# Hybrid encoder step on one core: z of block 0 leaves PSUM by ScalarE, two query loads in place of eight, the last gate norm dealt between attention heads

## The chip, the cores and the metric

The kernel runs on one core of one Trainium2 chip. The time is the device time of one execution in microseconds (us), the median of several executions. TensorE (PE in the profile, PEld for its weight loads) multiplies matrices into PSUM, VectorE (DVE), ScalarE (ACT) and GpSimd (POOL) work element by element, and SyncE (SP) issues all DMA transfers of this kernel from one queue.

## The reference

One layer of a streaming encoder with 2048 new frames of one stream ("prompt") and 32 further frames of another stream that has 2048 cached positions ("sample"). Model width is 1024.

```python
h = x + rmsnorm(mixer(rmsnorm(x, g_mix_pre)), g_mix_post)
y = h + rmsnorm(conv_ffn(rmsnorm(h, g_ffn_pre)), g_ffn_post)

# mixer
proj = h @ w_in                       # q, k, v (8 heads x 64), z (512), x/B/C (768), dt (8)
attn = stick_breaking(q, k_all, v_all)      # w = sigmoid(z_qk) * prod of (1 - sigmoid) of later keys
y = ssd_scan(silu(dwconv(xbc)), softplus(dt), ...) + d_skip * x
y = rmsnorm(y * silu(z), g_ssm_out)         # the gate and the gate norm
out = concat([rmsnorm(attn, g_attn_out), y]) @ w_out
# conv_ffn
act = gelu(dwconv(gate)) * up;  out = act @ w_down
```

The results are both y, the new k and v rows, and the final scan and convolution states. Everything is float32; the kernel splits an operand into a high and a low part and takes three matmuls for a product.

## The kernel before, in words

The 2080 frames are cut into four blocks (`SBS`): three of 512 prompt frames, and a last one of 512 prompt frames and the 32 sample frames (544). Features lie on the partitions, frames on the free axis.

`phase_in` runs over the four blocks: input norm, the projections of x/B/C, v, k and q, the SSD scan, and for blocks 0 to 2 also the gate and its norm. In `gate`, each of four chunks of 128 features is a dense product of 24 matmuls in a PSUM bank named o (two banks, `kn.po`). The chunk's z is then put through a sigmoid, multiplied with itself and into the scan's output `xc`. Block 0 differs: its input norm factor r0 is not yet multiplied into x, so each projection is multiplied by r0 when it leaves PSUM. For z, VectorE does this at line 647 straight from the bank; blocks 1 and 2 copy z out by ScalarE at line 651 and need no factor. `gate_norm` then squares and sums the four chunks (lines 667 to 671), gets the reciprocal root, scales each chunk on VectorE (line 677), splits it (lines 681, 683) and stores the parts in DRAM (`yS`, lines 684 and 685).

A z chunk can only start when its bank is free, so with two banks the third chunk waits until the first has left PSUM.

Block 3's gate and gate norm are handed out as two generators (line 619). They run in the next stage, the attention of block 0. `Attention.heads` goes through "slots", one for each head, key block and 128 queries: 32 slots for block 0 (8 heads x 1 key block x 4), 64 for block 1, and so on. A slot computes scores on PE (lines 890, 894; tile z), two sigmoids on ScalarE (738, 739; gam and beta), a running product by a scan on VectorE (741), a product of these (746; POOL, or VectorE for one in five), transposes on PE (909; pt), a split by ScalarE and VectorE (913, 914; wt), and the value matmuls (931; pa). Between slots `fill` takes steps from a generator `filler`, at a rate of `steps / slots`. For block 0 the filler is block 3's gate: 32 steps of six matmuls each (128 x 256 or 272 wide), one a slot. At every third slot a step of `sample` (the sample frames' attention over the cached keys) is taken as well, ten in all. `sample` begins with a memset of its query tile qp on VectorE (761), then SP loads qp from DRAM, one load for each head (764), then the first keys (786). When the heads of block 0 are done, the rest of `sample` and the whole of block 3's gate norm follow.

Then `Tail` begins: block 0's attention output is normed (`norm_in`, lines 832 to 839), goes with yS through the output projection, a residual and a second norm, and the feed-forward, all as filler between the slots of block 1's heads.

The order of instructions on each engine is set by the tile framework's scheduler when the program is built. It may move an instruction ahead of others that it does not depend on. Filler matmuls are pinned behind the last attention matmul that was recorded before them (`pin`, `mark`); attention slots are not pinned behind filler, so the scheduler can take slots of the next heads first where it expects the filler to wait. On the chip each engine works through its list in order.

Of the kernel before, what the change touches and what calls it, by code (L numbers as in the profile page):

```python
# [8 lines left out]
F32 = mybir.dt.float32  # L9
# [3 lines left out]
ALU = mybir.AluOpType  # L13
# [18 lines left out]
P = 128  # L32
D = 1024
KC = D // P
SEQ = 2048
DEC = 32
# [228 lines left out]
def phase_in(kn, ctx):  # L265
# [101 lines left out]
    for s, (t0, nt) in enumerate(SBS):  # L367
# [250 lines left out]
        if last:  # L618
            return lambda tm, pool: (
                gate(kn, s, xs, xc, None, tm),  # L620
                gate_norm(kn, s, xc, tm, lambda sq, *r: kn.rstd_narrow(pool, *kn.bank, [sq], *r)),
            )
        bufs = {"khi": 2, "klo": 2, "t": 2, "sq": 1, "zc": 2}
        tm = lambda nm: (so if nm in ("khi", "klo") else tmp).tile([P, 550 if nm == "t" else 544], F32, name=nm, bufs=bufs[nm])
# [6 lines left out]
def gate(kn, s, xs, xc, r0, tm):  # L631

    nc, nt = kn.nc, SBS[s][1]
    tiles = tiles_of(nt)
    for c in range(4):
        w = kn.weight(kn.wp, kn.a["wz"][c], key=("z", c) if s < NSB - 1 else ("z", c, "part"))
        for c0, c1 in tiles:
            n = c1 - c0
            ps = kn.po.tile([P, 512], F32, name="o")
            for k in range(KC):  # L640
                kn.dense(ps, w[k : k + 1], xs, c0, c1, k0=k, first=k == 0, last=k == KC - 1, pin=s == NSB - 1)
                if len(tiles) == 1 or k % 2:
                    yield
            t = tm("t")
            if r0 is not None:
                z = tm("t")
                nc.vector.tensor_tensor(z[:, :n], ps[:, :n], r0[:, c0:c1], op=ALU.mult)
                ps = z
            elif s < NSB - 1:
                z = tm("zc")  # L650
                nc.scalar.copy(z[:, :n], ps[:, :n])
                ps = z
            nc.scalar.activation(t[:, :n], ps[:, :n], AF.Sigmoid)
            nc.vector.tensor_tensor(t[:, :n], ps[:, :n], t[:, :n], op=ALU.mult)
            e = min(c1, 512)
            nc.vector.tensor_tensor(xc[:, c, c0:e], xc[:, c, c0:e], t[:, : e - c0], op=ALU.mult)
            if c1 > 512:
                nc.gpsimd.tensor_tensor(xc[:, c, 512:544], xc[:, c, 515:547], t[:, e - c0 : n], op=ALU.mult)


def gate_norm(kn, s, xc, tm, rstd):

    nc, nt = kn.nc, SBS[s][1]
    sq = tm("sq")
    for c in range(4):
        if c == 0:
            nc.scalar.activation(sq[:, :nt], xc[:, c, :nt], AF.Square)
        else:
            t = tm("t")
            nc.scalar.activation(t[:, :nt], xc[:, c, :nt], AF.Square)  # L670
            nc.gpsimd.tensor_tensor(sq[:, :nt], sq[:, :nt], t[:, :nt], op=ALU.add)
        yield
    r = rstd(sq, nt, 512)
    for c in range(4):
        yield
        n = xc[:, c, :nt] if s == NSB - 1 else tm("zc")[:, :nt]
        nc.vector.scalar_tensor_tensor(
            n, xc[:, c, :nt], kn.col(C_GSSM + c), r[:, :nt], op0=ALU.mult, op1=ALU.mult
        )
        hi = tm("khi")[:, :nt].bitcast(F32R)  # L680
        nc.scalar.copy(hi, n)
        lo = tm("klo")[:, :nt].bitcast(F32R)
        nc.gpsimd.tensor_tensor(lo, n, hi.bitcast(F32), op=ALU.subtract)
        nc.sync.dma_start(kn.yS[s][0, :, c, :], hi.bitcast(F32))
        nc.sync.dma_start(kn.yS[s][1, :, c, :], lo.bitcast(F32))


class Attention:
# [60 lines left out]
    def sample(self, ctx, pu):  # L749
        kn, nc, a = self.kn, self.kn.nc, self.kn.a  # L750
        kp = ctx.enter_context(kn.tc.tile_pool(name="as_k", bufs=2, reuse_waits="tile", side="right"))
        mk = kp.tile([P, DEC], BF16, name="masks", bufs=1)
        nc.gpsimd.memset(mk[:], 0.0)
        for i in range(4):
            r = slice(32 * i, 32 * i + 32)
            nc.gpsimd.affine_select(
                out=mk[r, :], in_=mk[r, :], compare_op=ALU.is_gt, fill=NEG, base=0,
                pattern=[[-1, DEC]], channel_multiplier=1,
            )
        qp = kp.tile([P, 4, DH], F32, name="qp", bufs=1)  # L760
        nc.vector.memset(qp[:], 0.0)
        for h in range(NH):
            r = slice(64 * (h % 2), 64 * (h % 2) + 64)
            nc.sync.dma_start(qp[r, h // 2, 32 * (h % 2) : 32 * (h % 2) + 32], kn.qF[r, h // 2, :])
        own = []
        for g in range(2):
            own.append([kp.tile([P, w], F32, name=f"{nm}{g}", bufs=1) for nm, w in (("sgam", 513), ("sbeta", 512), ("sprow", 513))])
            nc.gpsimd.memset(own[g][0][:, 512:513], 1.0)
        carry = [kp.tile([P, 1], F32, name=f"scarry{g}", bufs=1) for g in range(2)]
        av = pu.tile([P, 512], F32, name="u")  # L770
        prev = [None, None]
        for kc in (4, 3, 2, 1, 0):
            n = DEC if kc == 4 else 512
            nsub = 1 if kc == 4 else 4
            v = [kp.tile([P, 512], F32, name="sv", bufs=4) for _ in range(nsub)]
            for i in range(nsub):
                if kc == 4:
                    nc.sync.dma_start(v[i][:DEC, :], kn.vF[:])
                else:
                    nc.sync.dma_start(v[i][:], a["cvv"][:, 4 * kc + i, :])  # L780
            for g in range(2):
                z = self.pz.tile([P, 512], F32, name="z")
                for i in range(2):
                    c = 2 * g + i
                    k = kp.tile([P, 512], F32, name="sk", bufs=2)
                    nc.sync.dma_start(
                        k[:, :n], kn.kF[:, c, :] if kc == 4 else a["ck"][c][:, 512 * kc : 512 * kc + 512]
                    )
                    nc.tensor.matmul(
                        z[DH * i : DH * i + DH, :n], qp[:, c, :], k[:, :n], start=True, stop=kc < 4  # L790
                    )
                if kc == 4:
                    nc.tensor.matmul(z[:, :n], kn.identb[:], mk[:], start=False, stop=True)
                w, end = self.weights_of(z[:, :n], n, prev[g], own[g])
                prev[g] = carry[g][:]
                nc.scalar.copy(prev[g], end)
                t = self.pt.tile([P, 512], F32, name="pt")
                q = min(n, P)
                for i in range(nsub):
                    nc.tensor.transpose(t[:q, P * i : P * i + P], w[:, P * i : P * i + q], kn.ident[:])  # L800
                wt = kp.tile([P, 512], F32, name="swt")
                nc.scalar.copy(wt[:q, : nsub * P], t[:q, : nsub * P])
                for i in range(nsub):
                    for e in range(2):
                        nc.tensor.matmul(
                            av[DH * e : DH * e + DH, P * g : P * g + P], wt[:q, P * i + DH * e : P * i + DH * e + DH],
                            v[i][:q, 256 * g + P * e : 256 * g + P * e + P],
                            start=kc == 4 and g == 0, stop=kc == 0 and g == 1 and i == 3, skip_group_check=True,
                        )
                yield  # L810
        self.att_s = self.cp.tile([P, 4, DEC], F32, name="att_s")
        for g in range(2):
            at = kp.tile([P, DH], F32, name="at")
            for hh in range(4):
                r = slice(32 * hh, 32 * hh + 32)
# [683 lines left out]
def build(nc, tc, a, o):  # L1499
    kn = Kernel(nc, tc, a, o)  # L1500
    with ExitStack() as ctx:
# [24 lines left out]
        att = Attention(kn, heads)  # L1526
        kn.bank = pu, "u"
        late = ssd.enter_context(tc.tile_pool(name="ssd_tmp", bufs=2, reuse_waits="tile", side="right"))
        att.filler, normed = rest(lambda nm: late.tile([P, 544], F32, name=nm, bufs=1 if nm == "sq" else 2), late)
        with ExitStack() as c2:  # L1530
            sample = att.sample(c2, pu)

            out = att.heads(0, KC * 4, lambda i: i % 3 == 2 and next(sample, None))
            for _ in sample:
                pass
        for _ in normed:
            pass
        ssd.close()
        tail = Tail(kn, att, ctx, pu)
        for s in range(NSB):  # L1540
# [106 lines left out]
```

## Time and profile before

| | |
|---|---|
| median of 3 executions | 2916.16 us (2910.6 to 2920.89) |
| the profiled execution | 2923.02 us |
| its span, first to last instruction | 2921.2 us |
| mean granted PE clock | 0.98 of full |
| PE busy | 2806.3 us |
| VectorE, ScalarE, POOL busy | 1636.6, 1221.8, 1151.0 us |

The profile is of one execution. Its times in us count from the start of the span. The groups by line give an operation with its busy time, mean duration and the idle time before it, with the instruction whose end released it ("<-DVE t L647"). In the timeline a row is start, length, engine, line, operation and count, and in brackets the idle time before it. The windows give the busy time of every engine in a stretch, then the granted PE clock, the DMA engines' share and GB/s. The input phase takes up to about 606 us, the heads of block 0 from there to about 715 us.

### The profile page before, as it was taken

To read this page: it belongs to the slowest core of one execution; us is meant where nothing else is said; L and a number is where in the kernel's file an instruction comes from. 1 tells how busy PE (TensorE), PEld (TensorE's weight loads), DVE (VectorE), ACT (ScalarE), POOL (GpSimd) and SP (SyncE) were. 2 spreads that over 40 slices of the span, in tenths; PEclk is the share of its full clock that TensorE was granted. 3 is DMA by queue.
4 is the path that set the end of the run, shared out by engine and by line. 5 is a ranking of instruction groups with operands and counts; after the bars stand their busy time and mean duration, and the time that the engine had idled before them with its cause. 6 is when DMAs were issued, how large, how long until landed. Compare 5 with 4: busy or idle time off the path is not lost.

```text
span 2921.2 us, 46172 instructions
## 1 busy us (share of the span) xinstructions
PE 2806.3 (96%) x16771; PEld 2427.1 (83%) x16771; DVE 1636.6 (56%) x2628; ACT 1221.8 (42%) x2575; POOL 1151.0 (39%) x1076
## 2 busy tenths in 40 slices
PE   7989999979899999999899999989999999999998
PEld 6768889967878888897788888978888889899997
DVE  7584747448664545457454556776666653623333
ACT  4343434247665545455333334654444443321211
POOL 4634242225766656555322223453322323411113
PEclk9999999999989999999999999999999999999999
DMA  7878776868677777785655556666555555755556
GB/s 270 266 267 245 238 241 205 235 191 289 241 249 256 267 275 257 254 284 186 211 176 175 183 181 227 205 197 200 171 164 172 169 167 189 238 180 180 170 177 205
DMA packets 336708, 632.08 MB, mean 216 GB/s; under 512 B 73594, under 2 KB 193026, under 8 KB 328162
## 3 DMA queue, kind: packets, MB, share of 16 engines
q1 hardware_dynamic: 336482, 629.13, 66.4%
q8 instruction: 134, 2.20, 0.3%
q14 instruction: 92, 0.75, 0.1%
HBM read 472.44 MB, written 156.57 MB: 215 GB/s over the span
## 4 chain that ended last, share of the span: by engine, by line
PE 78%; DMA 9%; DVE 7%; SPq 2%; ACT 2%; issue 2%; POOL 1%; DVEq 0%; ACTq 0%; POOLq 0%
PE o L173 39%; PE u L173 12%; PE t L173 11%; PE z L890 4%; PE pa L931 4%; PE pt L909 3%; PE o L432 3%; DMA acB<-acD 2%; DMA w<-wS_out 1%; DVE prow L741 1%; DMA xr<-hS 1%; DMA wraw<-wbx 1%; DVE xlo L1079 1%; DMA o_kT<-kf 1%; PE u L215 1%
## 5 line engine op out<-in xcount | busy, mean ns | idle before, releaser
L173 PE MATMUL o<-xhi,w 128*128 128x512 f32 (+2 forms) x3968 | 1047.2, 345 | 28.8 <-ACT xhi L346 7.7
L173 PEld LDWEIGHTS o<-xhi,w 128*128 128x128 f32 x3968 | 698.1, 191 | 121.6 <-issue 10.8
L173 PE MATMUL o<-xlo,w 128*128 128x512 f32 (+2 forms) x1984 | 683.0, 344 | 3.0 <-DVE xlo L1079 1.6
L746 POOL TENSOR_TENSOR beta<-beta,prow 128x512 f32<-128x512 f32 (+3 forms) x256 | 255.4, 998 | 448.2 <-DVE prow L741 365.8
L173 PEld LDWEIGHTS o<-xlo,w 128*128 128x128 f32 x1984 | 379.4, 191 | 46.7 <-DVE xlo L1079 2.4
L173 PE MATMUL o<-ah,w 128*128 128x512 f32 x992 | 345.0, 404 | 8.2 <-DVE f L1375 6.8
L173 PE MATMUL u<-xhi,w 128*128 128x512 f32 x1056 | 348.7, 397 | 0.0
L154 POOL TENSOR_TENSOR w<-wraw,w 128x512 fp32r<-128x512 f32 (+3 forms) x189 | 253.8, 1346 | 163.9 <-ACT w L153 143.0
L1327 POOL TENSOR_TENSOR y<-y,gb 128x512 f32<-128x512 f32 (+1 forms) x88 | 115.9, 1317 | 508.4 <-ACT gb L1326 508.2
L914 DVE TENSOR_TENSOR wt<-pt,wt 128x512 fp32r<-128x512 f32 (+2 forms) x320 | 191.2, 601 | 170.3 <-ACT wt L913 168.2
L741 DVE TENSOR_TENSOR_SCAN prow<-gam,prow,z 128x513 f32<-128x513 f32 x192 | 245.1, 1277 | 60.9 <-ACT beta L739 57.1
L913 ACT CAST wt<-pt 128x512 fp32r<-128x512 f32 (+2 forms) x320 | 167.1, 526 | 220.6 <-PE pt L909 219.3
L173 PEld LDWEIGHTS u<-xhi,w 128*128 128x128 f32 x1056 | 198.8, 188 | 46.7
L173 PEld LDWEIGHTS o<-ah,w 128*128 128x128 f32 x992 | 187.7, 189 | 50.6 <-DVE f L1375 8.3
L738 ACT ACTIVATE gam<-z 128x512 f32<-128x512 f32 (+2 forms) x320 | 172.7, 540 | 100.2 <-PE z L890 57.0
L173 PE MATMUL u<-xlo,w 128*128 128x512 f32 x528 | 209.3, 396 | 0.0
L173 PE MATMUL o<-al,w 128*128 128x512 f32 x496 | 197.2, 398 | 0.0
L173 PE MATMUL t<-xhi,w 128*128 128x272 f32 x960 | 189.2, 293 | 2.8 <-DMA w<-wS_up 1.8
L153 ACT CAST w<-wraw 128x512 fp32r<-128x512 f32 (+3 forms) x189 | 117.5, 622 | 169.2 <-PE o L173 103.5
L931 PE MATMUL pa<-wt,v 128*64 128x256 f32 (+3 forms) x1152 | 174.1, 282 | 11.6 <-DVE wt L914 10.6
L909 PE MATMUL pt<-ident,beta 128*128 128x128 f32 x1088 | 180.9, 278 | 2.3 <-DVE wt L914 1.9
L1319 DVE SCALAR_TENSOR_TENSOR y<-gb,cv,y 128x512 f32<-128x512 f32 (+1 forms) x176 | 142.2, 808 | 68.4 <-ACT y L1317 65.9
(285 smaller groups left out, 4899.5 us busy)
## 6 DMA issues: line engine op xcount, KB each, us to landing
w<-wS_up SPq DMA_DIRECT2D x264, 512.0 KB, 3.5
w<-wS_dn SPq DMA_DIRECT2D x144, 384.0 KB, 3.5
wS_up<-w SPq DMA_DIRECT2D x88, 512.0 KB, 3.5
w<-wS_out SPq DMA_DIRECT2D x78, 512.0 KB, 6.1
wraw<-wup SPq DMA_DIRECT2D x88, 256.0 KB, 4.1
k<-kS SPq DMA_DIRECT2D x80, 256.0 KB, 3.8
v<-vS SPq DMA_DIRECT2D x80, 256.0 KB, 3.7
wS_dn<-w SPq DMA_DIRECT2D x48, 384.0 KB, 3.1
```

What stands on the lines that cost most here:

```text
L153: nc.scalar.copy(hi, raw[:, :m, :])
L154: nc.gpsimd.tensor_tensor(lo, raw[:, :m, :], hi.bitcast(F32), op=ALU.subtract)
L173: mm = nc.tensor.matmul(ps[:, : c1 - c0], l, r, start=first and i == 0 and k == 0, stop=last and i == 2 and k == len(w) - 1, **({"skip_gro ...
L738: nc.scalar.activation(g[:, c0:512], z, AF.Sigmoid, scale=-0.125)
L741: nc.vector.tensor_tensor_scan(back(pr), back(g), z[:, 0:1].to_broadcast([P, n + 1]), self.kn.ones[:, 0:1] if prev is None else prev, op0= ...
L746: eng.tensor_tensor(b[:, :n], b[:, :n], pr[:, c0 + 1 : 513], op=ALU.mult)
L890: mm = nc.tensor.matmul(z[:, :n], q[:, P * b : P * b + P], k[:, :n], start=e == 0, stop=e == 1 and kc < s)
L909: mm = nc.tensor.transpose(t[:, P * j : P * j + P], w[:, P * j : P * j + P], kn.ident[:])
L913: nc.scalar.copy(hi, t)
L914: nc.vector.tensor_tensor(lo, t, hi.bitcast(F32), op=ALU.subtract)
L931: nc.tensor.matmul(av[:m, 2 * P * p + c0 : 2 * P * p + 2 * P], v[:, j, :m], wt[:, rest, j, c0:], start=kc == s and p + j + rest == 0, stop ...
L1319: nc.vector.scalar_tensor_tensor(y[:, :W], gb[:, i : i + W], kn.col(wc + i), y[:, :W], op0=ALU.mult, op1=ALU.add)
```

## The change

Three edits; line numbers in the changed file are the same or a few lower:

1. In `gate`, block 0 now also copies z out of PSUM by ScalarE (into a tile zc) and multiplies by r0 on VectorE in place, from zc.
2. `sample` loads qp by two transfers, each of 64 partitions with all four head pairs (64x4x32), in place of eight of 64x32.
3. Block 3's gate norm is chained behind its gate as filler of block 0's heads. The number of steps is 44 in place of 32, so the filler runs at 1.375 steps a slot. The norm's steps are four for the squares, four empty ones (`rests`) behind the reciprocal root, and four for the scalings. Its two small PSUM tiles come from the banks named o in place of the bank named u.

```diff
-                gate_norm(kn, s, xc, tm, lambda sq, *r: kn.rstd_narrow(pool, *kn.bank, [sq], *r)),
+                gate_norm(kn, s, xc, tm, lambda sq, *r: kn.rstd_narrow(pool, kn.po, "o", [sq], *r), 4),
...
-            if r0 is not None:
-                z = tm("t")
-                nc.vector.tensor_tensor(z[:, :n], ps[:, :n], r0[:, c0:c1], op=ALU.mult)
-                ps = z
-            elif s < NSB - 1:
+            if s < NSB - 1:
                 z = tm("zc")
                 nc.scalar.copy(z[:, :n], ps[:, :n])
+                if r0 is not None:
+                    nc.vector.tensor_tensor(z[:, :n], z[:, :n], r0[:, c0:c1], op=ALU.mult)
                 ps = z
...
-def gate_norm(kn, s, xc, tm, rstd):
+def gate_norm(kn, s, xc, tm, rstd, rests=0):
...
     r = rstd(sq, nt, 512)
+    for _ in range(rests):
+        yield
...
-        for h in range(NH):
-            r = slice(64 * (h % 2), 64 * (h % 2) + 64)
-            nc.sync.dma_start(qp[r, h // 2, 32 * (h % 2) : 32 * (h % 2) + 32], kn.qF[r, h // 2, :])
+        for e in range(2):
+            r = slice(DH * e, DH * e + DH)
+            nc.sync.dma_start(qp[r, :, DEC * e : DEC * e + DEC], kn.qF[r, :, :])
...
-        att.filler, normed = rest(lambda nm: ..., late)
+        att.filler = chained(*rest(lambda nm: ..., late))
...
-            out = att.heads(0, KC * 4, lambda i: i % 3 == 2 and next(sample, None))
+            out = att.heads(0, KC * 4 + 12, lambda i: i % 3 == 2 and next(sample, None))
             for _ in sample:
                 pass
-        for _ in normed:
-            pass
```

**ScalarE's list at block 0's gate.** Before (the two casts are the weights of z chunks 2 and 3, xhi is block 1's input split):

```order
L260 COPY rstd<-st 128x512
L153 CAST w<-wraw 128x1024 x2
L653 ACT_TABLE_LOAD
L653 ACTIVATE t<-t 128x512
L667 ACTIVATE sq<-xc 128x512
L653 ACTIVATE t<-t 128x512
L153 CAST w<-wraw 128x1024
L331 CAST xhi_1603<-x 128x512
```

Now, with the sigmoid's line at 651 and the new copy at 647:

```order
L260 COPY rstd<-st 128x512
L153 CAST w<-wraw 128x1024
L647 COPY zc<-o 128x512
L153 CAST w<-wraw 128x1024
L651 ACT_TABLE_LOAD
L651 ACTIVATE t<-zc 128x512
L647 COPY zc<-o 128x512
L651 ACTIVATE t<-zc 128x512
L665 ACTIVATE sq<-xc 128x512
L153 CAST w<-wraw 128x1024
L647 COPY zc<-o 128x512
L331 CAST xhi_1607<-x 128x512
```

The first chunk's copy stands ahead of a weight cast, but the second chunk's copy stands behind the first chunk's sigmoid, which needs VectorE's product with r0.

**SP's list where `sample` begins.** Before and then now:

```order
L778 DMA sv<-vF 32x512
L764 DMA qp<-qF 64x32 x8
L786 DMA sk<-kF 128x32 x2
L885 DMA k<-kS_78 128x512
L145 DMA w<-wS_z_0_1446 128x2x512
```

```order
L778 DMA sv<-vF 32x512
L764 DMA qp<-qF 64x4x32 x2
L786 DMA sk<-kF 128x32 x2
L885 DMA k<-kS_78 128x512
L145 DMA w<-wS_z_0_1447 128x2x512
```

Six issues are gone from between the sample's first values and its first keys; nothing else has moved in front of them.

**PE's list in the last heads of block 0**, one slot with the scores over 384 and one over 512 keys. Before, with the six gate matmuls of a filler step ahead of a pair of slots:

```order
L173 MATMUL o<-xhi_4228,w 128x272
L890 MATMUL z<-k,qa 128x384
L890 MATMUL z<-k,qb 128x384
L894 LDWEIGHTS identb
L894 MATMUL z<-maskq,identb 128x128
L890 MATMUL z<-k,qa 128x512
L890 MATMUL z<-k,qb 128x512
L805 MATMUL u<-sv,swt 64x128 x8
L909 MATMUL pt<-ident,beta 128x128 x4
L173 MATMUL o<-xhi_7263,w 128x256
```

Now, at the same pair of slots:

```order
L215 MATMUL o<-ones,sq 128x1 x4
L215 MATMUL o<-ones,sq 32x1
L931 MATMUL pa<-wt,v 128x256
L931 MATMUL pa<-wt,v 128x128
L931 MATMUL pa<-wt,v 64x256
L931 MATMUL pa<-wt,v 64x128
L890 MATMUL z<-k,qa 128x384
L890 MATMUL z<-k,qb 128x384
L894 LDWEIGHTS identb
L894 MATMUL z<-maskq,identb 128x128
L890 MATMUL z<-k,qa 128x512
L890 MATMUL z<-k,qb 128x512
```

The gate matmuls of these slots have gone to earlier slots: the last of them stands in the 26th slot, and the 8 slots behind it have no filler matmuls. The norm's sums (line 215) stand in the 30th slot. From the 35th slot to the first long run of output projection matmuls there are 10 slots rather than 17.

**VectorE's list around the four scalings of the gate norm** (line 677). Before, in the first slots of block 1's heads:

```order
L914 TENSOR_TENSOR wt<-pt,wt 128x4x128
L741 SCALAR_TENSOR_TENSOR prow<-gam_5845,ones,z 128x385
L677 SCALAR_TENSOR_TENSOR xc<-xc,cv,rstd 128x544 x4
L914 TENSOR_TENSOR wt<-pt,wt 128x4x128
L228 TENSOR_SCALAR rn_v<-u 128x2
```

Now, where block 0's heads end and block 1's begin (sprow is the sample's scan):

```order
L946 TENSOR_TENSOR att<-pa,att 64x512
L914 TENSOR_TENSOR wt<-pt,wt 128x2x128
L677 SCALAR_TENSOR_TENSOR xc<-xc,cv,rstd 128x544 x4
L741 SCALAR_TENSOR_TENSOR sprow_6001<-sgam_5999,scarry_6004,z 128x513
L741 SCALAR_TENSOR_TENSOR prow<-gam_5848,ones,z 128x129
```

The four scalings still stand as one piece, about ten slots earlier, now with the sample's scan directly behind them.

More of the change, by code (lines that the diff above doesn't have):

```diff
@@ L1528, in build @@
         late = ssd.enter_context(tc.tile_pool(name="ssd_tmp", bufs=2, reuse_waits="tile", side="right"))
-        att.filler, normed = rest(lambda nm: late.tile([P, 544], F32, name=nm, bufs=1 if nm == "sq" else 2), late)
+        att.filler = chained(*rest(lambda nm: late.tile([P, 544], F32, name=nm, bufs=1 if nm == "sq" else 2), late))
         with ExitStack() as c2:
             sample = att.sample(c2, pu)
-            out = att.heads(0, KC * 4, lambda i: i % 3 == 2 and next(sample, None))
+            out = att.heads(0, KC * 4 + 12, lambda i: i % 3 == 2 and next(sample, None))
             for _ in sample:
                 pass
-        for _ in normed:
-            pass
         ssd.close()
```

## The prediction

> **What bounds the kernel now.** I read the page's summary first, then what PE waited for in the stretches that the change touches.
>
> ```profile
> span 2921.2 us, 46172 instructions
> PE 2806.3 (96%) x16771; PEld 2427.1 (83%) x16771; DVE 1636.6 (56%) x2628; ACT 1221.8 (42%) x2575; POOL 1151.0 (39%) x1076
> ```
>
> PE is the bound, and its work is untouched. So the change can only win idle time of PE (2921.2 - 2806.3 = 115 us in all) and matmuls that run at a reduced clock behind such idle time. Three of the waits that PE is listed with belong to the three edits:
>
> ```profile
> PE o L173 <- DVE t L647: 6.0, 1, 6.0
> PE z L789 <- DMA sk<-kF: 7.0, 1, 7.0
> PE pa L931 <- DVE wt L914: 4.8, 1, 4.8
> ```
>
> ```profile
> core 0: us, PE busy (x) PEld busy (x) DVE busy (x) ACT busy (x) POOL busy (x), PEclk, DMA share, GB/s
> 606.00:640.00 34.00, 22.25 (x146) 18.98 (x145) 15.81 (x30) 16.55 (x46) 9.12 (x19) 0.85 0.72 224
> 640.00:715.00 75.00, 71.96 (x541) 54.61 (x542) 55.28 (x87) 53.10 (x133) 35.94 (x42) 1.00 0.86 277
> 715.00:755.00 40.00, 31.29 (x175) 26.13 (x175) 34.27 (x56) 24.29 (x57) 28.77 (x29) 0.79 0.61 208
> ```
>
> The heads of block 0 (606 to 715 us) wait at their start and are then PE-bound (72.0 of 75 us). The first slots of block 1's heads, 715 to 755 us, lose 8.7 us of PE idle and, at clock 0.79, about 0.21 x 31.3 = 6.6 us of slowed matmuls.
>
> **Edit 1, block 0's z.** Rows of the timeline around it, engine by engine, and the last two from the chain of waits:
>
> ```profile
> 152.62 7.46 DVE L322 SCALAR_TENSOR_TENSOR x<-x,cv,rstd 128x512 f32<-128x512 f32 x8
> 160.00 0.68 DVE L647 TENSOR_TENSOR t<-o,r 128x512 f32<-128x512 f32 x1
> 154.59 1.28 ACT L653 ACT_TABLE_LOAD   x1
> 160.71 0.63 ACT L653 ACTIVATE t<-t 128x512 f32<-128x512 f32 x1 [4.84 <-DVE t L647]
> 183.45 0.57 ACT L397 COPY raw<-o 128x512 f32<-128x512 f32 x1
> 160.82 0.77 PE L173 MATMUL o<-xhi,w 128*128 128x512 f32 x1 [5.97 <-DVE t L647]
> 149.37 2.38 POOL L154 TENSOR_TENSOR w<-wraw,w 128x1024 fp32r<-128x1024 f32 x1 [4.04 <-ACT w L153]
> 176.43 1.88 DVE L332 TENSOR_TENSOR xlo<-x,xhi 128x512 fp32r<-128x512 f32 x3
> 178.33 3.05 SPq L311 DMA_DIRECT2D x<-xT  x4
> 165.07 2.70 POOL L154 TENSOR_TENSOR w<-wraw,w 128x1024 fp32r<-128x1024 f32 x1 [7.53 <-ACT w L153]
> 193.59 0.47 PE L173 MATMUL o<-xhi,w 128*128 128x512 f32 x1 [2.32 <-DMA w<-wS_bx]
> 182.00 11.46 DMA w<-wS_bx
> 201.83 11.39 PE o L173 x48
> ```
>
> PE stands still from 154.85 to 160.82 because VectorE reads the first z bank only behind eight products of the next block's norm (L322). ScalarE is idle in that time, and its copy (0.6 us, as L397) now stands ahead of them: the bank is free before 154.9, and chunk 2's weights are split at 149.37 + 2.38 = 151.8. So chunk 2 starts 6.0 us earlier. The wait does not vanish, however. The second chunk's copy stands behind the first sigmoid, which still needs VectorE's product at 160.0 to 160.7: sigmoid to 161.3, copy to 161.9. Chunk 2 ends at 154.9 + 5.7 (half of 48 matmuls in 11.39) = 160.6, so chunk 3 waits some 1.4 us. That leaves 4.6 us. VectorE's splits of block 1's input (L332) start without waiting for chunk 2 and end at about 173.5 to 174 rather than 178.3; they free the buffer into which SP loads 2 MB of x at 178.33. Behind that load stands the next thing that is late, the recalled weights (182.00, 11.46 us to land, PE waiting 2.3 us at 193.59). If the load moves by 4 to 5 us, so do the weights. If instead the store in front of the recall sets it, which hangs on casts that still follow VectorE's product at 160, only 1 to 2 us remain. Four copies of 0.6 us on an idle ScalarE cost nothing here; without that cover they would be 2.4 us. I take **-4**, bounds -7 (the whole wait, and a first matmul of 0.47 us rather than 0.77, as the rows show, and a few like it) and -1.
>
> The in-place product is not in the trace. Its nearest rows are two with tiles of the same size:
>
> ```profile
> L656 DVE TENSOR_TENSOR xc<-xc,t 128x512 f32<-128x512 f32 x4 | 4.8, 1212 | 0.1
> L647 DVE TENSOR_TENSOR t<-o,r 128x512 f32<-128x512 f32 x4 | 2.7, 682 | 2.5 <-PE o L173 2.5
> ```
>
> From PSUM it takes 0.68 us, and L656, with both inputs in SBUF, takes 1.21 in the mean of the same stretch. I take 0.7, since POOL is idle for 7.5 us before 165.07, when the one on the path runs.
>
> The Trainium skill has a rule that speaks against this edit: "SBUF — State Buffer", section "Who interferes with whom", says that a VectorE instruction with two SBUF inputs is blocked by a GpSimd instruction that reads SBUF, for the whole of it. The rows above agree (1212 against 682 ns). By the rule each product could take half a us more, the sum for this edit -3.5, and this part's answer would be the same.
>
> **Edit 2, the query loads.**
>
> ```profile
> 615.75 0.27 DVE L761 MEMSET qp<- 128x256 f32 x1
> 616.05 4.92 SPq L764 DMA_DIRECT2D qp<-qF  x8
> 621.01 1.06 SPq L786 DMA_DIRECT2D sk<-kF  x2
> 621.64 1.55 DMA sk<-kF
> 623.18 0.39 PE L789 MATMUL z<-sk,qp 128*64 128x32 f32 x2 [6.97 <-DMA sk<-kF]
> L764 SPq DMA_DIRECT2D qp<-qF x8: 444/595/596, 616.1 to 620.4; - x8
> 641.83 0.81 PE o L173 x6
> L130 SPq DMA_DIRECT2D wraw<-wz x4: 339/811/1420, 119.4 to 146.9; - x4
> ```
>
> SP cannot start before VectorE's memset, which does not move. Eight issues take 4.92 us, 0.615 each, and the first keys are issued behind them. Six fewer: 6 x 0.615 = 3.7 us, so the keys land at about 619.5. The faster filler also puts one more gate step (six matmuls, 0.81 us) ahead of the waiting matmul, inside the wait. The wait goes from 7.0 to 7.0 - 3.7 - 0.8 = 2.5 us. The wide load is not in the trace; other issues of SP here take 0.3 to 1.4 us. At 1.4 each the saving is 2.1; a landing 0.6 later leaves 1.5. The other bound is -6, if PE's restart is also faster. I take **-4**. Queued behind qp on SP are the keys, block 0's next k and the gate's weights; all come earlier.
>
> Rows that show the restart:
>
> ```profile
> 608.99 0.44 PE L890 MATMUL z<-k,qa 128*128 128x384 f32 x1 [2.15 <-DVE prow L741]
> 612.28 0.66 PE L173 MATMUL o<-xhi,w 128*128 128x272 f32 x2
> 634.49 0.42 PE L173 MATMUL o<-xhi,w 128*128 128x272 f32 x2
> ```
>
> After a wait of only 2.15 us a pair of matmuls takes 0.66 us, against 0.42 at 634, still 3.3 us later. So I count no faster restart from a wait of 2.5 us.
>
> The Trainium skill, "TensorE: Matmul & The Clock Gate", section "What's actually happening", has the clock halved after an idle window of about 3.4 us; a wait of 2.5 us would then escape and save about 1.7 us more (4.5 us of matmuls at 0.66 for 0.42). The row at 612.28 disagrees, so it stays in the bound; by the rule edit 2 would give -5.7.
>
> **Edit 3, the gate norm.** PE's work does not change; what changes is which slots have filler. In 640 to 715 there are 25 slots (3.0 us each), in 715 to 755 16 (2.5 us):
>
> ```profile
> L890 PE MATMUL z<-k,qa 128*128 128x512 f32 (+3 forms) x25 | 9.4, 377 | 1.3 <-DVE sprow L741 1.3
> L890 PE MATMUL z<-k,qa 128*128 128x512 f32 (+3 forms) x16 | 7.9, 493 | 1.5 <-DVE prow L741 1.3
> 733.76 5.43 DVE L677 SCALAR_TENSOR_TENSOR xc<-xc,cv,rstd 128x544 f32<-128x544 f32 x4
> 739.85 1.11 PE L931 MATMUL pa<-wt,v 128*64 128x256 f32 x4 [4.75 <-DVE wt L914]
> PE z L789 <- DMA sk<-ck: 1.1, 2, 0.7
> ```
>
> Gain: a slot without filler wasted (8.7 + 6.6) / 16 = 0.96 us, and by the new order 10 rather than 17 of them stand between the heads' seam and the output projection, since the norm's chain, its stores and its casts are out of the way. 7 x 0.96 = 6.7 us; the wait of 4.75 us behind the four scalings is among it. Loss: 8 slots at the end of block 0's heads lose their filler. Such a slot has 3.0 - 0.8 = 2.2 us of work for PE. For VectorE it has 55.3 / 25 = 2.2, less 0.2 for the gate's products, plus (5.4 + 0.3) / 8 = 0.7 for the norm: 2.7. So VectorE sets it, and PE wastes 0.5 us, 4.0 in 8 slots. Net 4.0 - 6.7 = **-2.7**, call it -3. The bounds: no waste in the 8 slots, -7; the waste of the slots behind the seam and again a wait of 4.75 us behind the scalings, 7.7 + 4.8 - 6.7 = +6. ScalarE and POOL stay below VectorE there (53.1 / 25 = 2.1 and 1.4 us a slot). SP gets the norm's eight stores earlier, behind loads that have landed by then.
>
> **Sum.** -4 - 4 - 3 = -11 us on the profiled execution: 2923.0 (1.8 of it outside the span) goes to 2912. The median of the runs shown is 2916.2, 6.9 below the profiled one, and the gaps are the same in each, so the forecast is 2905.
>
> **Rivals.** *Given back to transfers.* The recalled weights after block 0 do not come earlier, and the sample's key loads, in a stretch with a DMA share of 0.86, set the pace behind the shortened wait: edit 1 gives -1, edit 2 -1.5 and edit 3 -3, so -5.5, 2911. For it: the recall takes 11.46 us to land, and PE already waits for it. Against: PE loses only 1.1 us to the cached keys' loads (the last row above). *The uncovered slots cost what the others gain.* The 8 slots waste 0.96 us each and the scalings again stop PE: edit 3 at +6, in all -2, 2914. For it: the scalings still stand as one piece, now with the sample's scan behind them. Against: there are sample matmuls to run meanwhile. *Slower.* The norm's chain (squares, sums, POOL's root, PE's spread, scalings, splits) stretches the seam slots through VectorE's list, since each later score matmul waits for a scan. With edits 1 and 2 at -8 and the 7 saved slots, it decides from a waste of (8 + 6.7 + 8.8) / 8 = 2.9 us a slot, three times that seen: 2925. *More.* The restarts are faster and the 8 slots cost nothing: -7 - 6 - 7 = -20, 2896. That the edits do not do what they say is ruled out for the order, which is above; a wide qp load that is no cheaper is in edit 2's bound.
>
> **How the numbers follow.** A difference within 0.3% (8.7 us) can't be told from none. Forecast 0.54 (between 2899 and 2909, nine tenths of it below 2907.4), transfers 0.18, uncovered slots 0.14, slower 0.05, more 0.09. Faster: 0.48 + 0.09 + 0.02 of the transfers' case = 0.59; slower 0.05; the same 0.36. The bounds of the unknown costs add up to -20 and +3.5, 2896 to 2920. All of them at one end at once is unlikely, above all at the upper end, where it takes the uncovered slots and the transfers together; below, the median of the runs may fall 2 us lower. The range is 2894 to 2917, which leaves out the slower case and a part of "more" and of the two others.
>
> **What would show it.** Right: PE's wait for L647 gone, one of 1 to 2 us in its place, and the x load at about 174; z L789 waiting some 2.5 us with two qp issues; fewer PE idle us from 715 to 755, and 0.5 us a slot lost ahead of it. Wrong: a longer wait at the recalled w, qp issues of over 1 us, or PE waiting over 5 us behind the four scalings again.

## The result, and the profile after

The changed kernel takes 2901.59 us in the median of 8 executions (2896.59 to 2905.92), the kernel before 2918.79 in the median of 8. The ratio comes out at 0.995, with a 95% interval of 0.9935 to 0.9966: 14.6 us less, between 10 and 19. (The two medians are 17.2 us apart, which lies within it; in the experiments too a ratio can differ from that of the medians by up to 0.001.) The forecast was 2905 and faster. The profiled execution of after took 2896.59 us and is the fastest of its eight, that of before (2923.02) stands near the upper end of its own, so the two traces differ by 26 us; some 12 us of that are the spread of executions. Of all executions that are quoted below one, the profiled one of the last kernel of the experiments, was disturbed (5459 us): its ratio leaves it out, and no trace of it is read.

The summary of the page after:

```profile
span 2894.6 us, 46186 instructions
PE 2796.1 (97%) x16771; PEld 2414.0 (83%) x16771; DVE 1641.2 (57%) x2628; ACT 1224.8 (42%) x2579; POOL 1142.5 (39%) x1076
```

PE works 10 us less at the same 16771 matmuls (fewer of them at a reduced clock), and its idle time falls from 115 to 98.5 us.

The rows of the timeline that answer to the prediction's first two edits, in the kernel after:

```profile
160.30 0.50 PE L173 MATMUL o<-xhi,w 128*128 128x512 f32 x1 [1.48 <-ACT zc L647]
172.18 0.50 PE L173 MATMUL o<-xlo,w 128*128 128x512 f32 x1 [2.42 <-DVE xlo L332]
192.09 0.47 PE L173 MATMUL o<-xhi,w 128*128 128x512 f32 x1 [2.75 <-DMA w<-wS_bx]
177.34 2.71 SPq L311 DMA_DIRECT2D x<-xT  x4
617.79 0.27 PE L789 MATMUL z<-sk,qp 128*64 128x32 f32 x2 [2.37 <-DMA sk<-kF]
614.30 1.19 SPq L764 DMA_DIRECT2D qp<-qF  x2
```

The wait of 5.97 us for L647 has become one of 1.48 us, as forecast. But 12 us later there is a new wait of 2.42 us for the low part of block 1's input, the x load stands at 177.3 and not at 174, and the recalled weights are as late as before (2.75 us, before 2.32). The wait for the first keys is 2.37 us (forecast 2.5).

To see where the time went, the start of the matmul at the same place of PE's list is compared in both traces, and the list is cut at seven such places. Where two lists differ in order, the matmul at the same place need not be the same one. So the cuts lie where the lists have done the same matmuls so far, to within 0.3 us of work (0.9 at 690 us for the row "rate 36"; an estimate from the median spacing of each kind of matmul in three of the traces). The length of each piece against the kernel before is, in us (negative is shorter; the head row gives the times in the trace of before):

```
                     0-150 150-200 200-614 614-690 690-811 811-1301 1301-1600 1600-end
full change           -1.6    0.1    -0.5    -9.0    -2.8      1.1     -7.6     -6.6
edit 1 alone          -1.1    0.7    -1.9     0.1    -0.5      2.0      1.3     -2.9
edit 2 alone          -2.2   -0.5    -3.4    -7.0    -1.7     -1.5     -8.1     -5.4
edit 3 alone          -1.3   -2.9     0.7    -4.0    -1.9      1.2     -4.4    -10.5
edits 2 and 3         -1.6   -0.2     1.1    -9.3    -2.0      0.8     -5.0      0.3
two loads, old order  -1.9    0.1     0.1    -4.0    -0.3      1.4      0.7    -10.0
six loads             -1.4    0.2     0.8    -3.7    -4.1     -0.9    -10.5    -10.6
edit 1, VectorE split -2.1   -6.6     3.8    -0.1    -0.3      0.1      0.1     -4.9
edit 3, old rate      -1.7   -1.4    -1.3    -0.1    -6.9      1.5     -9.9     -7.1
edits 2, 3, rate 36    0.8   -6.5     0.7    -8.0    -5.5      1.3    -12.3     -8.2
edit 1, no POOL read  -1.3   -8.5    -1.0    -0.4    -3.5      0.1      0.0     -3.1
before, no POOL read  -0.5   -6.2     0.4    -0.5    -3.2     -0.5      0.0     -7.3
```

The rows below the first are the experiments of the next section. In the last column nearly the whole of PE's list is the same in all kernels, and still it runs from +0.3 to -10.6: that is how far two executions of one list differ there, and the one of before is slow. In the other columns a difference of 1 to 3 us says little either, and in 150-200 one of 6 us can be chance (the last section comes back to it).

Two places stand out. From 614 to 811 us, the place of edits 2 and 3, the full change gains 11.8 us. And the piece 1301-1600, the seam from block 1's heads to block 2's, touches none of the edited lines and still gains 7.6. The windows of the two kernels there, cut at the same places, and the two around edit 3 ahead of it; first before:

```profile
690.00:715.00 25.00, 24.44 (x201) 19.92 (x200) 19.73 (x36) 20.30 (x51) 14.33 (x17) 1.00 0.94 307
715.00:760.00 45.00, 36.28 (x216) 30.99 (x217) 35.46 (x58) 29.19 (x70) 33.02 (x35) 0.81 0.58 196
1301.10:1600.20 299.10, 283.08 (x1419) 233.28 (x1419) 167.80 (x239) 120.63 (x274) 111.50 (x113) 0.98 0.60 194
```

and after:

```profile
679.00:712.60 33.60, 28.98 (x201) 21.00 (x200) 24.41 (x36) 23.17 (x57) 24.09 (x25) 0.95 0.95 322
712.60:747.00 34.40, 30.36 (x217) 25.47 (x216) 25.96 (x55) 26.04 (x61) 23.43 (x26) 0.95 0.58 187
1288.40:1580.00 291.60, 282.67 (x1419) 232.51 (x1420) 168.82 (x242) 122.17 (x275) 106.55 (x112) 0.98 0.60 196
```

Edit 3 does what was forecast in kind: the last slots of block 0 grow by 8.6 us (25.0 to 33.6), the first of block 1 shrink by 10.6 (45.0 to 34.4); up to 1 us of either is another mix of matmuls, by the same estimate. In the far piece as many matmuls keep PE busy as long as before (283.1 and 282.7 us), and what is won is PE's idle time, 16.0 to 8.9 us. Here the change moves PE's instructions: compared without buffer numbers, PE's lists of before and after differ in order from 615 us to 1599, that is to the end of this seam, since the scheduler takes heads and filler in another turn from the sample's start on. Behind it they are the same, but for some 20 matmuls at 2421 to 2425 us.

The place of a cut matters. At 1150 us PE's list after is 4.0 us of matmuls ahead of before's at the same place (2.3 with edit 2 alone). A cut there would show 12.5 us won behind it and 5.2 lost from 760 us on, most of which is work that changed sides. The expectations below speak of 1150 to 1600 us; where they are answered, the pieces of the table stand for it.

### The profile page after: what moved, and what is told of

Same layout as the page of the kernel before. It is cut to its first block, busy times and chain, and to the rows that moved or that the text cites. A ratio compares the mean times of both kernels' runs of the same rounds, so it can differ in the third digit from the quotient of the medians.

```text
span 2894.6 us, 46186 instructions
## 1 busy us (share of the span) xinstructions
PE 2796.1 (97%) x16771; PEld 2414.0 (83%) x16771; DVE 1641.2 (57%) x2628; ACT 1224.8 (42%) x2579; POOL 1142.5 (39%) x1076
## 4 chain that ended last, share of the span: by engine, by line
PE 83%; DVE 6%; DMA 5%; ACT 2%; issue 2%; POOL 1%; SPq 1%; DVEq 0%; ACTq 0%; POOLq 0%
PE o L173 42%; PE u L173 12%; PE t L173 11%; PE z L890 4%; PE pa L931 4%; PE pt L909 3%; PE o L432 3%; DVE prow L741 1%; DMA wraw<-wbx 1%; DVE xlo L1079 1%; DMA o_kT<-kf 1%; DMA acB<-acD 1%; DMA xr<-hS 1%; DMA w<-wS_out 1%; PE u L215 1%
```

## The experiments

Ratios are against the kernel before on the same chip, with their 95% intervals. The kernels ran on three chips, so ratios and not times are compared from one group to another. Traces of before that are quoted are the one of the prediction.

**Each edit alone, and two without the third.** The edits are those of the diff above, nothing else.

> Only edit 1 (block 0's z copied out by ScalarE). Theory: the 6 us that PE wins at the third z chunk are given back some 12 us later, because VectorE's two-input products of this stretch stand still while POOL splits weights; so a ratio of 0.9995 (within 0.2%), PE waiting over 2 us for xlo L332 near 172 us, the x load within 1.5 us of where it stood before (178.3), and the wait of 2 to 3 us for the recalled weights kept. Rival (the prediction's term): -4 us, ratio 0.9986, the x load at 174 and the recalled weights 4 us earlier.

> Only edit 2 (two query loads). Theory: the saving is the six issues of 0.6 us plus a wait of the value load or a faster restart behind it, -5 to -9 us, ratio 0.997 to 0.998; PE's wait for the first keys falls from 7.0 to about 3.3 (without the extra filler step). Rival (the prediction's term, issues alone): -3.7 us, ratio 0.9987.

> Only edit 3 (gate norm in steps). Theory: what the stretch from 715 to 755 us wins, the slots without filler before it lose, within 2 us at 850 us; what is won comes later, with another order between the heads of blocks 1 and 2, -4 to -8 us at the end, ratio 0.997 to 0.9986. Rival (the prediction's term): -3 us at 850 us and nothing behind it, ratio 0.999. Second rival: nothing at all, 1.000.

> Edits 2 and 3 without edit 1. Theory (edit 1 is worth nothing): the ratio of the full change, 0.995, within 0.001. Rival (edit 1 is worth its -4): 0.9964.

| kernel | median, us | ratio | interval |
|---|---|---|---|
| edit 1 alone | 2916.61 | 1.000 | 0.9986 to 1.0014 |
| edit 2 alone | 2894.63 | 0.9926 | 0.991 to 0.9942 |
| edit 3 alone | 2903.15 | 0.9957 | 0.9942 to 0.9973 |
| edits 2 and 3 | 2899.91 | 0.9943 | 0.9926 to 0.9961 |

Edit 1 is worth nothing, as the first theory had it; the rival's 0.9986 is the very edge of the interval, but the x load stands at 177.87 and PE waits 2.4 us for xlo, as the theory said (and 3.6 us for the recalled weights, where it had 2 to 3). Edit 2 alone comes out higher than the whole change (21.6 us against 14.6, with intervals that overlap) and higher than either theory of it allowed. Edits 2 and 3 do not add up, and the two without edit 1 stand where the whole change stands (the rival's 0.9964 is just outside the interval). Edit 3 alone comes out higher than its theory, whose 0.997 the interval just reaches, and than both rivals. By the table, edit 2 alone has 7.0 us at its own place, 3.2 behind it up to 1301 us and 8.1 from 1301 to 1600; edit 3 alone has 5.9 from 614 to 811 (its theory had that within 2 us of nothing) and 4.4 in the same far stretch, as the theory had it. Nearly half of either gain up to 1600 us comes from a place that the edit does not touch.

**Is the far gain the order, or the shorter wait?** Two kernels take edit 2's query loads apart from the order that follows. The first has edit 2 and three loads that nothing uses, behind the first two keys:

```diff
+                    if kc == 4 and (g, i) == (1, 1):
+                        qd = kp.tile([DH, 4, DEC], F32, name="qd", bufs=1)
+                        for h in range(3):
+                            nc.sync.dma_start(qd[:, h % 4, :], kn.qF[0:DH, h % 4, :])
```

With it PE's list from 705 us on is that of before, but for one pair of matmuls at 2423 us. The second has six loads in place of eight, two of them 64x2x32; from 811 us on its PE list is that of edit 2 alone.

```diff
-        for h in range(NH):
...
+        for i in range(6):
+            e = i % 2
+            h = slice(0, 2) if i < 2 else slice(1 + i // 2, 2 + i // 2)
...
```

> Only edit 2, with three unused query loads behind the first two keys, so that the first keys come as early as with edit 2, while all engines keep the order of the kernel before from 665 us on (with edit 2 alone PE's list differs over 900 rows up to 1600 us). Theory (most of edit 2's gain is the other order of block 1's slots and its filler): the local 6 us alone, ratio 0.9975 to 0.9985, and no gain between 1150 and 1600 us. Rival (the gain comes from the shorter wait and what it moves in time): as edit 2 alone, 0.9926.

> Six query loads in place of eight: two issues fewer, 1.2 us, but PE's list behind the stretch of the sample's start is the one of edit 2 alone. Theory (order): 12 us between 1150 and 1600 us as in edit 2 alone, and some 3 to 4 us less than that at the sample's start, ratio 0.993 to 0.995. Rival (issues): -1 to -2 us, ratio 0.9995.

Two loads in the old order: 2914.62 us, 0.9988 (0.9975 to 1.0001). Six loads in the new order: 2896.48 us, 0.9935 (0.9918 to 0.9953). So by the ratios the order is worth some 18 us (21.6 less 3.5, or 19.0 less the 1.2 of two issues) and the six issues in the old order some 4, each uncertain by 4 to 6 us. The windows of the piece 1301-1600, in the kernel with the old order and then in the one with six loads:

```profile
1296.40:1596.20 299.80, 282.88 (x1420) 232.88 (x1419) 166.17 (x239) 120.64 (x274) 110.99 (x113) 0.98 0.62 194
```

```profile
1292.00:1580.60 288.60, 279.95 (x1419) 230.64 (x1418) 167.00 (x243) 122.14 (x276) 106.13 (x110) 0.99 0.63 200
```

The former is the row of before again (299.10, 283.08). The rival, that the shorter wait moves something in time, falls.

What the old order does there can be seen in the timeline of before; VectorE's rows and the two matmuls that wait:

```profile
1390.82 0.43 DVE L1411 TENSOR_TENSOR f<-f,xr 128x256 f32<-128x256 f32 x1 [4.21 <-DMA xr<-hS]
1394.58 1.52 DVE L1411 TENSOR_TENSOR f<-f,xr 128x256 f32<-128x256 f32 x1 [2.73 <-DMA xr<-hS]
1397.82 0.13 DVE L232 SCALAR_TENSOR_TENSOR rn_v<-u,rcol 128x2 f32<-128x2 f32 x1
1397.95 0.80 PE L890 MATMUL z<-k,qa 128*128 128x512 f32 x1 [5.22 <-DVE rn_v L232]
1401.95 1.01 PE L931 MATMUL pa<-wt,v 128*64 128x256 f32 x4 [2.04 <-DVE wt L914]
```

VectorE's residual adds (L1411) stand in its list ahead of the scan and of the small L232 that PE's next scores need, and wait for their loads from DRAM; PE stands 5.22 us behind them. In the kernel after, the matmuls of that place wait for less:

```profile
1372.47 0.73 PE L931 MATMUL pa<-wt,v 128*128 128x256 f32 x4 [2.51 <-ACT wt L913]
1374.75 1.22 PE L250 MATMUL u<-ident,rn_v 128*128 128x128 f32 x4 [1.55 <-POOL rn_v L238]
```

VectorE waits about as long for these loads in both (15.1 and 13.2 us), but PE no longer stands behind them as long. These rows are 3.2 of the 7.1 us of PE's idle time that is won (5.22 and 2.04 against 2.51 and 1.55); the rest is spread over smaller waits, of at most 1.3 us less each, and was not taken apart. That the residual adds are the cause is read from these rows: no kernel here moves them alone.

**The same order by another way, and a further order.** Edit 3 alone at one filler step a slot leads to the list of edit 2 alone from 1125 us on; edits 2 and 3 at 36 steps lead to an order of their own up to some 1450 us.

```diff
-            out = att.heads(0, KC * 4 + 12, lambda i: ...)
+            out = att.heads(0, KC * 4 + 0, lambda i: ...)     # edit 3 alone
+            out = att.heads(0, KC * 4 + 4, lambda i: ...)     # edits 2 and 3
```

> Edit 3 alone with the filler at its old rate of one step a slot, so that the gate covers all 32 slots and the norm's steps follow the heads; PE's list from some 1100 us on is that of edit 2 alone, reached by an edit elsewhere. Theory (that order is worth 12 us whatever leads to it): -10 to -14 us between 1150 and 1600 us, ratio 0.9945 to 0.9965. Rival (the query loads themselves made those 12 us): nothing there, ratio 0.999 to 1.001.

> Edits 2 and 3 with 36 filler steps in place of 44; PE's list from 1100 us on is a further one, neither that of before, of edit 2 nor of the full change. Theory: every such order has its own price, so the local part alone is foreseeable, -6 us (0.998), and the stretch from 1150 to 1600 us may be anything from 0 to -13. Rival (the order before is the odd one out, the others agree): -9 to -13 us there as well, ratio 0.993 to 0.995.

Edit 3 at the old rate: 2896.54 us, 0.9941 (0.9922 to 0.9961), and -9.9 us in the piece 1301-1600 (its theory had 10 to 14), beside -8.1 and -10.5 for the two kernels that come to this order by edit 2: the order has its price whatever leads to it. With 36 steps: 2890.66 us, 0.9918 (0.99 to 0.9936). The window of the far piece in this kernel:

```profile
1283.90:1570.70 286.80, 280.02 (x1419) 230.38 (x1419) 166.31 (x242) 121.52 (x274) 106.52 (x111) 0.99 0.62 200
```

It is 12.3 us shorter, near the upper end of what both theories allowed there, and the whole gain is larger than either had; the price of an order was not foreseen, only that it has one. All three other orders are better there than that of before: by 4.4 to 7.6 us (the full change's, in three kernels), 8.1 to 10.5 (edit 2's, in three) and 12.3. So the old order is the odd one out, as the rival said.

**Where edit 1's gain goes.** The timeline of after, VectorE and then POOL:

```profile
163.82 2.51 DVE L649 TENSOR_TENSOR zc<-zc,r 128x512 f32<-128x512 f32 x1 [0.60 <-ACT zc L647]
168.67 2.85 DVE L654 TENSOR_TENSOR xc<-xc,t 128x512 f32<-128x512 f32 x1
171.44 4.66 DVE L332 TENSOR_TENSOR xlo<-x,xhi 128x512 fp32r<-128x512 f32 x4
163.39 2.40 POOL L154 TENSOR_TENSOR w<-wraw,w 128x1024 fp32r<-128x1024 f32 x1 [8.08 <-PE o L173]
168.54 2.43 POOL L154 TENSOR_TENSOR w<-wraw,w 128x1024 fp32r<-128x1024 f32 x1 [2.75 <-ACT w L153]
173.09 2.47 POOL L154 TENSOR_TENSOR w<-wraw,w 128x1024 fp32r<-128x1024 f32 x1 [2.12 <-ACT w L153]
```

Products that take 0.68 us alone last 2.5 and 2.9 us, each beside one of POOL's weight splits, and end some 0.5 us behind it. The r0 products of the first two chunks come too early for that; the third (L649) does not, and edit 1 made it a product of two SBUF tiles. Before, the split at 165.07 fell into 2.5 us in which VectorE stood idle, and only the next one, at 171.94, met splits of x (three of them took 4.10 us). With edit 1 all three splits meet products, and the splits of x (L332), which PE needs next, are late by all of this. Two kernels take POOL's reads away, by clearing the low part of these three weight chunks in place of computing it, with edit 1 and without:

```diff
-        nc.gpsimd.tensor_tensor(lo, raw[:, :m, :], hi.bitcast(F32), op=ALU.subtract)
+        if key in (("bx", 4, 0), ("bx", 5, 0), ("bx", 0, 0)):
+            nc.gpsimd.memset(lo.bitcast(F32), 0.0)
+        else:
+            nc.gpsimd.tensor_tensor(lo, raw[:, :m, :], hi.bitcast(F32), op=ALU.subtract)
```

> Edit 1 alone, and POOL clears the low part of three weight chunks of block 1 (L154 there, no read of SBUF) rather than computing it: this leaves out those low parts. Theory (VectorE's two-input products wait for POOL's splits): no such product takes over 0.8 us between 160 and 178 us, PE's wait of 2.4 us for xlo goes, the x load stands at 174 or earlier, and at 195 us PE is 3 to 6 us ahead of the kernel with edit 1 alone. Rival (transfers set the pace): products short, but PE no more than 1 us ahead at 195 us.

> The kernel before with the same low parts left out, as the other half of the comparison. Theory: here PE is held by its wait for L647 up to 161 us, so the cleared parts win less, 1 to 3 us at 195 us; edit 1 is then worth 3 to 5 us at that point. Rival: edit 1 is worth no more than 1 us here either.

With edit 1 every product from 160 to 172 us takes 0.7 us, the x load stands at 171.4, PE's wait for xlo is 0.2 us, that for the recalled weights 1.1, and PE is 8.5 us ahead over the piece 150-200. Without edit 1 it is 6.2 us ahead there, where 1 to 3 were expected. The rows bear out the theory of where the gain went: with POOL's reads the products stretch, without them they do not. The sizes are less certain. In both executions the eight products of L322 took 5.4 us and not 7.5 (last section), and the piece 150-200 varies by over 6 us even between kernels that leave block 0's gate and these splits as they were before. Edit 1's own worth is 2.3 us here, less than the 3 to 5 expected, since the wait for L647 that it removes was only 3.87 us in this execution; the times of these two single executions (2905.64 and 2905.37) do not tell them apart.

A third kernel leaves nothing out: VectorE computes these low parts, so POOL does not read.

```diff
+        if key in (("bx", 4, 0), ("bx", 5, 0), ("bx", 0, 0)):
+            nc.vector.tensor_tensor(lo, raw[:, :m, :], hi.bitcast(F32), op=ALU.subtract)
+        else:
...
```

> Edit 1 alone, with the low parts of three weight chunks of block 1 computed by VectorE rather than POOL; nothing is left out. Theory (VectorE's standing behind POOL's reads eats edit 1): three splits of some 1.3 us each on VectorE cost less than the 5 to 6 us that its products stood still, so no product over 0.8 us there, and PE 2 to 5 us ahead of the kernel with edit 1 alone at 200 us; in the time -2 to -4 us, ratio 0.9986 to 0.9995. Rival: VectorE's added work delays the low parts of x as much as the standing did, 1.000.

Edit 1 with it takes 2910.49 us, 0.9988 (0.9976 to 1.000). VectorE's rows there:

```profile
162.59 1.23 DVE L155 TENSOR_TENSOR w<-wraw,w 128x1024 fp32r<-128x1024 f32 x1
163.73 0.68 DVE L652 TENSOR_TENSOR zc<-zc,r 128x512 f32<-128x512 f32 x1
168.48 2.49 DVE L335 TENSOR_TENSOR xlo<-x,xhi 128x512 fp32r<-128x512 f32 x4
```

The split takes 1.23 us and ends POOL's lock; the products are back at 0.68, the four splits of x at 2.49 (4.66 above), and the x load moves to 172.2. That is 6.6 us in the piece 150-200, of which 3.8 are given back by 614 us. By the interval edit 1 and the moved splits together are now worth 0 to 7 us, so the theory is borne out by the durations and only just by the time; no kernel moves the splits without edit 1, so its own share is not shown.

**The two together.** The same with edit 2:

> The same with edit 2, in the order that edit 2 alone gives. Theory: edit 2 alone and 2 to 4 us more, ratio 0.991 to 0.992, faster than both kernels. Rival: as edit 2 alone, 0.9926.

It takes 2887.85 us in the median of its five other executions, 0.9915 (0.9895 to 0.9934), against 0.995 (0.9935 to 0.9966) of the full change and 0.9926 of edit 2 alone; the interval does not tell it from the latter. With 36 filler steps and edits 2 and 3, the time is the same (0.9918).

## Why the prediction was right or wrong

The time and the sign came out, 3 us above the median and well inside the range, but in part by luck: one of the three terms was worth nothing, the two others more than forecast together, and the sum lacked a fourth.

- **Edit 1, -4: failed.** The first half held: the bank is free early, chunk 2 starts 6 us earlier, chunk 3 waits 1.48 us (forecast 1.4). The step that failed is that "VectorE's splits of block 1's input ... end at about 173.5 to 174 rather than 178.3". They end at 177.3 (and PE's list stood 1.6 us earlier already at 150 us), since three of POOL's splits block VectorE for 1.8 to 2.2 us each. The price of the in-place product, 0.7 us "since POOL is idle for 7.5 us before 165.07", held for the first two chunks and the last, not for the third. The sentence on the Trainium skill, "SBUF — State Buffer", section "Who interferes with whom", named the mechanism, and the traces agree with it in the rows above (2.51 and 2.85 us beside splits of 2.40 and 2.43). But the half us for each r0 product that gave the -3.5 was the wrong size, and for the wrong products. It came from the mean of the four products of L656, 1212 ns; three of them took 0.69 us and one 2.78, beside a split of POOL, all in the timeline of before:

```profile
178.94 2.78 DVE L656 TENSOR_TENSOR xc<-xc,t 128x512 f32<-128x512 f32 x1
178.19 2.98 POOL L154 TENSOR_TENSOR w<-wraw,w 128x1024 fp32r<-128x1024 f32 x1 [3.44 <-ACT w L153]
```

  So a product that meets a split loses some 2 us and the others nothing, and an earlier chunk put more of them in its way.
- **Edit 2, -4: mechanism right, mis-sized.** The wait came out at 2.37 (forecast 2.5), and without the extra filler step it is 3.30 us in the kernel with edit 2 alone, just the 3.7 us of six issues. The piece 614-690 is 7.0 us shorter there, though. One part that the term lacked is the rest of SP's queue: the next value load, for which PE waited 1.42 us, is no longer late. The first row is of before, the second of edit 2 alone:

```profile
632.04 0.27 PE L789 MATMUL z<-sk,qp 128*64 128x32 f32 x2 [1.42 <-DMA sv<-cvv]
```

```profile
613.23 0.27 PE L789 MATMUL z<-sk,qp 128*64 128x32 f32 x2 [3.30 <-DMA sk<-kF]
```

  Another is the clock: in this piece it is 0.95 before and 0.98 with edit 2 alone, and PE is busy for 2.6 us less. In the kernel with the unused loads PE does not wait for that value load either, but the clock stays at 0.95, and the piece is 4.0 us shorter, the forecast's figure. The forecast's premise that the clock also falls behind a wait of 2.5 us held, though for a shorter time (last section).
- **Edit 3, -3: about right in the sum, wrong in both parts.** The last slots of block 0 cost 8.6 us, not 4.0, so VectorE's 0.5 us a slot was half of the truth; the slots behind the seam won 10.6, not 6.7. The net of -2.0 is near the forecast's -2.7. From 614 to 811 us edit 3 brings 2.6 us on top of edit 2 (11.3 against 8.7), alone 5.9. The wait of 4.75 us behind the scalings is gone, as forecast, but a part of the rival that the scalings would stop PE again came true: the sample's scan, which now stands directly behind them, has a wait of its own in the kernel after.

```profile
708.39 0.39 PE L890 MATMUL z<-k,qa 128*128 128x256 f32 x1 [2.49 <-DVE sprow L741]
```
- **What was not in the sum:** -7.6 us between 1301 and 1600. The prediction looked at the order at the three places of the edits, and took it for the same behind them; of PE's list only the first slots of block 1 were looked at. The sign of the far order could not be read from the profile of before. Without it the change would be worth some 7 to 10 us (14.6 by the ratio or 17.2 by the medians, less 7.6), between the rival of the transfers (5.5) and the forecast (11).

So the forecast was right for partly wrong reasons: edit 1 was taken 4 us too high, edits 2 and 3 together some 5 too low (11.8 from 614 to 811, forecast 7), and 7.6 us were missing. These figures come from single traces: from 150 to 1600 us they have 18.7 us for the full change, 1.5 us more than the medians show and 4 more than the ratio.

## What to carry to other kernels

Where a scheduler sets the order, a small edit reshuffles what comes after it, here for almost 1000 us: compare the whole list of the bounding engine before pricing an edit by its own place, and when measuring, make a twin with the same local saving in the old order. Compare two traces only between places where both have done the same work. A copy that leaves PSUM by another engine turns its next product into one of two SBUF tiles; look at what POOL reads in the 10 us behind it, for products further down the list as well, and read the single rows: a mean of 1.2 us was three rows of 0.69 and one of 2.78. Six small DMA issues cost what they take on the queue, 0.6 us each, plus a late load that stood behind them (1.42 us of PE's time here).

## What the hardware showed

**VectorE and POOL lock each other out, in both directions, and not the same way in each execution.** With the same order up to there, POOL's split beside VectorE's eight products (L322) waited for them in one execution and made them wait in another. In the kernel with edit 3 alone:

```profile
151.32 5.38 DVE L322 SCALAR_TENSOR_TENSOR x<-x,cv,rstd 128x512 f32<-128x512 f32 x8
153.32 5.61 POOL L154 TENSOR_TENSOR w<-wraw,w 128x1024 fp32r<-128x1024 f32 x1 [2.87 <-ACT w L153]
157.44 0.76 PE L173 MATMUL o<-xhi,w 128*128 128x512 f32 x1 [3.89 <-DVE t L647]
```

There the wait for L647 is 3.89 us. In the profiled execution of before the eight products took 7.46, POOL's split 2.89 and the wait 5.97: 2.1 us of the wait that the prediction set out to win were this lock. The piece 150-200 differs by up to 6.7 us between executions without edit 1 and with POOL's splits as before (+0.2 to -6.5 in the table); how much of that is the lock was not taken apart. What decides it was not tried.

**The clock falls some time after a wait began, not at its end, and a short wait brings it down too.** Windows behind the wait for the first keys and behind the one for L232, both in the kernel before; the waits are of 6.97 and 5.22 us:

```profile
623.18:628.00 4.82, 4.82 (x21) 4.04 (x22) 2.15 (x5) 1.95 (x7) 0.28 (x1) 0.50 0.87 256
1397.95:1406.20 8.25, 6.21 (x25) 5.63 (x26) 6.91 (x9) 4.85 (x11) 4.71 (x5) 0.50 0.66 215
```

and after, behind the first keys' 2.37 us:

```profile
617.80:621.50 3.70, 3.33 (x19) 2.66 (x20) 1.35 (x3) 1.30 (x6) 0.27 (x1) 0.81 0.94 289
621.50:626.00 4.50, 4.50 (x31) 3.77 (x29) 1.02 (x1) 2.14 (x6) 0.87 (x1) 0.78 0.90 310
```

Behind the long waits the clock is at 0.50 from the first matmul on, for 4.8 and 8.3 us (the latter with a further wait of 2.04 us in it). Behind the short one it is full for some 2 us, and only then at half, to 623.5; the two windows lose 0.19 x 3.7 + 0.22 x 4.5 = 1.7 us, the long wait at the first keys lost 0.5 x 4.8 = 2.4. So a wait of 2.4 us costs 4.1, and one of 7.0 costs 9.4. The Trainium skill, "TensorE: Matmul & The Clock Gate", section "What's actually happening", has half clock after an idle window of about 3.4 us; here waits of 2.15 and 2.37 us were enough.
